# Row sums of a 16384 x 1024 array: the last eight rows as five runs instead of four, with pieces of two rows summed on ScalarE

## The chip, the cores and the metric

The kernel runs on one core of a Trainium2 chip. The time is what the device takes for one execution, in microseconds (us); the kernel before takes 160.38 us, the median of three runs (160.38 to 160.41). A profile is one such execution, recorded instruction by instruction; its span runs from the first to the last instruction of the program.

Three engines of the core matter here. VectorE (DVE in the profile) and ScalarE (ACT) do the sums; SyncE (SP) issues the loads and the last store. Each engine works through its own instructions in order and waits on semaphores; a DMA adds 16 to its semaphore once all of it has landed. TensorE (PE) and GpSimd (POOL) do nothing for the result.

## The reference

```
def setup_inputs():
    batch, seq, dim = 32, 512, 1024
    return {"x": np.random.randn(batch, seq, dim).astype(np.float32)}

def reference(x):
    return np.sum(x, axis=-1).astype(np.float32)
```

64 MiB are read, and one number is kept of each row of 1024 values: 16384 sums, 64 KiB.

## The kernel before

**Tiling.** The 16384 rows are spread over 128 partitions, 128 rows to each (`J`). They are cut into two regions of the array: the first 16 rows of every partition (`x_a`, `out_a`), and the other 112 (`x_b`, `out_b`). Within a region each partition's rows are contiguous in memory. `sums` holds one column for each of the 128 rows of a partition.

**Loads.** All are issued by SyncE (L99). The first load has 8 rows a partition (4 MB); it is moved to the very start of the program by `issue_first_load_at_entry`. Then come seven blocks of 16 rows (8 MB each) into three buffers in turn (L150 to L155). From the third block on, SyncE waits with `summed` until the block that used the buffer has been reduced (L153). The last eight rows, called rows 0 to 7 below, wait in the same way (L176) and then come as four runs, each a contiguous stretch of every partition's 8192 values (L178 to L183):

| run | values | what | goes to |
|---|---|---|---|
| 1 | 5632 | rows 0 to 4, left half of row 5 | buffer |
| 2 | 1792 | row 6, the first 768 values of row 7 | buffer, at its seventh row |
| 3 | 512 | right half of row 5 | `ends` |
| 4 | 256 | the last 256 values of row 7 | `ends` |

**Sums.** `vec` (L104) is one VectorE reduction over a whole block; the first load and blocks 0 to 5 are done so (L173 to L175). `halves` (L113) sums one stretch on VectorE: it adds the two halves of the stretch pair by pair and accumulates the result, so a row of 1024 is one operation of 512 pairs, followed by a short instruction that writes the accumulated sum. `act` (L129) sums one stretch on ScalarE: an activation that copies to PSUM (never read again, four places in turn, so that an activation waits for the fourth one before it) with an accumulated sum, and again a short instruction that writes the sum. Each adds one to `acts`.

Block 6, the last whole one, is divided: its first ten rows are summed by VectorE with `halves` (L193 to L195), its other six by ScalarE (L196, L197). Then the last eight rows:

- VectorE waits for run 1, sums the left half of row 5 into a column right behind the place of run 3 (L201, `carried`), and then rows 0, 1 and 2. It waits for run 2 and sums row 7's first 768 values into a column behind the place of run 4 (L218). Then it waits for run 3 and sums it with that column (257 pairs: 512 values, the carried sum, a zero) for row 5 (L221), and waits for run 4 and does the same for row 7 (129 pairs, L224), which sets `done`.
- ScalarE sums rows 3 and 4 out of run 1 and row 6 out of run 2 (L204 to L206). Behind these it waits for block 6's sums and for run 2, and issues two stores of all earlier sums (L212, L213).
- SyncE waits for `done` and for all of ScalarE's sums (L227, L228), stores the last 16 columns of `sums` (L229), and waits until they have landed; that ends the program.

There is no scheduler: the order on each engine is the order in which the function writes it.

Of the kernel before, what the change touches and what calls it, by code (L numbers as in the profile page):

```python
# [29 lines left out]
@with_exitstack  # L30
def kernel(
    ctx: ExitStack,
    tc: tile.TileContext,
    x: bass.AP,
    out: bass.AP,
):
    nc = tc.nc
    nc.at_finalize(issue_first_load_at_entry)

    tc.close()
    tc.compile()  # L43

    fp32 = mybir.dt.float32
    P = 128
    batch, seq, dim = x.shape
    rows = batch * seq
    J = rows // P
    BIG = 16  # L50
    x_r = x.flatten_outer_dims()
    out_r = out.rearrange("b s -> (b s)")
    ONE = BIG
    TWO = J - ONE

    def region(first, n):
        lo, hi = first * P, (first + n) * P
        return (
            x_r[lo:hi, :].rearrange("(p j) d -> p j d", j=n),
            out_r[lo:hi].rearrange("(p j) -> p j", j=n),  # L60
        )

    x_a, out_a = region(0, ONE)
    x_b, out_b = region(ONE, TWO)

    def rows_from(j, n):
        if j < ONE:
            return x_a[:, j : j + n, :]
        return x_b[:, j - ONE : j - ONE + n, :]

    last = J // BIG - 1
    tail = last * BIG
    FIRST = 8

    taken = (nc.sbuf_base + 31) // 32 * 32
    ctx.enter_context(nc.sbuf_tensor("unused", [P, -taken % 4096], mybir.dt.uint8))
    bufs = [
        ctx.enter_context(nc.sbuf_tensor(f"rows_{k}", [P, BIG * dim], fp32))
        for k in range(3)
    ]  # L80
    SIXTH, EIGHTH = 512, 768
    PAD = 64
    ends = ctx.enter_context(
        nc.sbuf_tensor("ends", [P, 2 * (dim + PAD) - SIXTH - EIGHTH], fp32)
    )
    sums = ctx.enter_context(nc.sbuf_tensor("sums", [P, J], fp32))
    unread = [
        ctx.enter_context(nc.psum_tensor(f"unread_{k}", [P, dim], fp32)) for k in range(4)
    ]

    def semaphore(name):
        return ctx.enter_context(nc.semaphore(name=name))

    def block_of(t, a, n):
        return t[:, a * dim : (a + n) * dim].rearrange("p (n d) -> p n d", d=dim)

    def load(dst, src, k):
        sem = semaphore(f"load_{k}")
        nc.sync.dma_start(out=dst, in_=src).then_inc(sem, 16)  # L99
        return sem  # L100

    summed = semaphore("summed")

    def vec(j, block):  # L104
        n = block.shape[1]
        return nc.vector.tensor_reduce(  # L106
            out=sums[:, j : j + n],
            in_=block,
            axis=mybir.AxisListType.X,
            op=mybir.AluOpType.add,  # L110
        )

    def halves(dst, src):  # L113
        n = src.shape[-1] // 2
        return nc.vector.tensor_tensor_reduce(  # L115
            out=src[:, :n],
            in0=src[:, :n],
            in1=src[:, n:],
            scale=1.0,
            scalar=0.0,  # L120
            op0=mybir.AluOpType.add,
            op1=mybir.AluOpType.add,
            accum_out=dst,
        )

    acts = semaphore("acts")
    n_acts = 0

    def act(j, src, landed=None):  # L129
        nonlocal n_acts  # L130
        if landed is not None:
            nc.scalar.wait_ge(landed, 16)
        if n_acts >= len(unread):
            nc.scalar.wait_ge(acts, n_acts - len(unread) + 1)
        nc.scalar.activation(  # L135
            out=unread[n_acts % len(unread)][:, :],
            in_=src,
            func=mybir.ActivationFunctionType.Copy,
            accum_out=sums[:, j : j + 1],
        ).then_inc(acts, 1)  # L140
        n_acts += 1

    t = bufs[0]
    block = block_of(t, 0, FIRST)
    landed = load(block, rows_from(tail, FIRST), "first")
    loads = [(landed, tail, block)]
    for g in range(last):  # L150
        t = bufs[(1 + g) % 3]
        if g > 1:
            nc.sync.wait_ge(summed, g - 1)  # L153
        block = block_of(t, 0, BIG)
        loads.append((load(block, rows_from(g * BIG, BIG), g), g * BIG, block))  # L155

    j = tail + FIRST
    t = bufs[(1 + last) % 3]

    rows5, left6 = block_of(t, 0, 5), t[:, 5 * dim : 5 * dim + SIXTH]
    c = 6 * dim
    row7, left8 = t[:, c : c + dim], t[:, c + dim : c + dim + EIGHTH]
    n6, n8 = dim - SIXTH, dim - EIGHTH
    right6, right8 = ends[:, :n6], ends[:, n6 + PAD : n6 + PAD + n8]
    whole6, whole8 = ends[:, : n6 + 2], ends[:, n6 + PAD : n6 + PAD + n8 + 2]
    left_sums = [w[:, -2:-1] for w in (whole6, whole8)]  # L170
    for w in (whole6, whole8):
        nc.vector.memset(w[:, -1:], 0.0)  # L172
    for landed, first, block in loads[:-1]:  # L173
        nc.vector.wait_ge(landed, 16)
        vec(first, block).then_inc(summed, 1)  # L175
    nc.sync.wait_ge(summed, last - 1)  # L176
    line = rows_from(j, 8).rearrange("p n d -> p (n d)")
    runs = ((t[:, : 5 * dim + SIXTH], 0), (t[:, c : c + dim + EIGHTH], 6 * dim),  # L178
            (right6, 5 * dim + SIXTH), (right8, 7 * dim + EIGHTH))
    five, seventh, sixth, eighth = (  # L180
        load(dst, line[:, at : at + dst.shape[-1]], f"run_{k}")
        for k, (dst, at) in enumerate(runs)
    )  # L183

    def sum_of(row):
        return sums[:, j + row : j + row + 1]

    paired = semaphore("paired")
    carried = semaphore("carried")
    landed, first, block = loads[-1]  # L190
    n_pairs = 10
    nc.vector.wait_ge(landed, 16)
    for q in range(n_pairs):  # L193
        op = halves(sums[:, first + q : first + q + 1], block[:, q, :])
    op.then_inc(paired, 1)  # L195
    for q in range(n_pairs, BIG):  # L196
        act(first + q, block[:, q, :], landed if q == n_pairs else None)  # L197
    n_early = n_acts

    nc.vector.wait_ge(five, 16)  # L200
    halves(left_sums[0], left6).then_inc(carried, 1)  # L201
    for q in range(3):
        halves(sum_of(q), rows5[:, q, :])
    for q in range(3, 5):  # L204
        act(j + q, rows5[:, q, :], five if q == 3 else None)
    act(j + 6, row7, seventh)  # L206

    early = semaphore("early")
    nc.scalar.wait_ge(acts, n_early)
    nc.scalar.wait_ge(paired, 1)  # L210
    nc.scalar.wait_ge(seventh, 16)
    nc.scalar.dma_start(out=out_b[:, : TWO - BIG], in_=sums[:, ONE : J - BIG]).then_inc(early, 16)  # L212
    nc.scalar.dma_start(out=out_a, in_=sums[:, :ONE]).then_inc(early, 16)  # L213
    nc.scalar.wait_ge(early, 32)

    done = semaphore("done")
    nc.vector.wait_ge(seventh, 16)
    halves(left_sums[1], left8).then_inc(carried, 1)  # L218
    nc.vector.wait_ge(sixth, 16)
    nc.vector.wait_ge(carried, 1)  # L220
    halves(sum_of(5), whole6)  # L221
    nc.vector.wait_ge(eighth, 16)
    nc.vector.wait_ge(carried, 2)
    halves(sum_of(7), whole8).then_inc(done, 1)  # L224

    stored = semaphore("stored")
    nc.sync.wait_ge(done, 1)  # L227
    nc.sync.wait_ge(acts, n_acts)  # L228
    nc.sync.dma_start(out=out_b[:, TWO - BIG :], in_=sums[:, J - BIG :]).then_inc(stored, 16)  # L229
    nc.sync.wait_ge(stored, 16)  # L230
# [30 lines left out]
```

## Time and profile before

| | us |
|---|---|
| median of three runs | 160.38 |
| the profiled execution | 160.36 |
| its span, first to last instruction | 159.0 (159.05) |
| VectorE busy | 121.7 |
| ScalarE busy | 10.9 |
| block 6 landed | 147.47 |
| VectorE's first and last operation on the last eight rows | 154.15, 157.48 |
| last store: issued, landed | 157.59, 159.01 |

The groups of operations by shape, VectorE's and then ScalarE's (the columns after the bar are busy time in us, the mean of one in ns, and idle time before them with what ended it):

```profile
L106 DVE TENSOR_REDUCE sums<-rows 128x16 f32<-128x16384 f32 x6 | 103.3, 17220 | 21.3 <-DMA rows<-in_x_dram 21.3
...
L115 DVE CUSTOM_DVE_ANT_0 rows<-rows 128x512 f32<-128x512 f32 x13 | 8.1, 689 | 2.2 <-DMA rows<-in_x_dram 2.2
```

```profile
L135 ACT ACTIVATE unread<-rows 128x1024 f32<-128x1024 f32 x9 | 9.1, 1014 | 145.1 <-DMA rows<-in_x_dram 145.1
L135 ACT ACTIVATION_READ_ACCUMULATOR unread<-rows 128x1 f32 x9 | 1.7, 187 | 0.0
```

In a timeline each line has the start in us, the length in us, the engine, the line of the kernel, the operation, and what it writes and reads; in square brackets stands how long the engine was idle before it, and what ended the wait. An engine with a q behind its name (SPq, ACTq) is that engine's issuing side. Operations of one engine can overlap a little: the next one starts while the one before it still writes. CUSTOM_DVE_ANT_0 is `halves`, ACTIVATE is `act`, and the READ_ACCUMULATOR behind each writes its sum.

### The profile page before, as it was taken

To read this page: it belongs to the slowest core of one execution; us is meant where nothing else is said; L and a number is where in the kernel's file an instruction comes from. 1 tells how busy PE (TensorE), PEld (TensorE's weight loads), DVE (VectorE), ACT (ScalarE), POOL (GpSimd) and SP (SyncE) were. 2 spreads that over 40 slices of the span, in tenths; PEclk is the share of its full clock that TensorE was granted. 3 is DMA by queue.
4 is the path that set the end of the run, shared out by engine and by line. 5 is a ranking of instruction groups with operands and counts; after the bars stand their busy time and mean duration, and the time that the engine had idled before them with its cause. 6 is when DMAs were issued, how large, how long until landed. Compare 5 with 4: busy or idle time off the path is not lost.

```text
span 159.0 us, 124 instructions
## 1 busy us (share of the span) xinstructions
DVE 121.7 (77%) x43; ACT 10.9 (7%) x19; POOL 0.2 (0%) x4
## 2 busy tenths in 40 slices
DVE  0009920199994999949999599986999679995986
ACT  3000000000000000000000000000000000000995
POOL 0000000000000000000000000000000000000000
DMA  7996996997989969969969969989799699698994
GB/s 264 478 577 264 527 527 264 527 445 346 527 379 412 527 280 511 527 264 527 527 264 527 511 280 527 429 363 527 313 478 527 264 527 527 264 527 354 425 394 162
DMA packets 2160, 67.18 MB, mean 422 GB/s; under 512 B 624, under 2 KB 752, under 8 KB 1008
## 3 DMA queue, kind: packets, MB, share of 16 engines
q1 hardware_dynamic: 1872, 67.12, 98.1%
q10 hardware_dynamic: 288, 0.06, 0.2%
HBM read 67.11 MB, written 0.07 MB: 422 GB/s over the span
## 4 chain that ended last, share of the span: by engine, by line
DMA 74%; DVE 24%; issue 0%; SPq 0%
DMA rows<-in_x_dram 74%; DVE sums L106 22%; DVE rows L115 2%; SPq L99 0%; DVE ends L115 0%; DVE sums L115 0%
## 5 line engine op out<-in xcount | busy, mean ns | idle before, releaser
L106 DVE TENSOR_REDUCE sums<-rows 128x16 f32<-128x16384 f32 (+1 forms) x7 | 112.0, 16001 | 31.7 <-DMA rows<-in_x_dram 31.7
L135 ACT ACTIVATE unread<-rows 128x1024 f32<-128x1024 f32 x9 | 9.1, 1014 | 145.1 <-DMA rows<-in_x_dram 145.1
L115 DVE CUSTOM_DVE_ANT_0 rows<-rows 128x512 f32<-128x512 f32 (+2 forms) x15 | 8.9, 662 | 2.6 <-DMA rows<-in_x_dram 2.6
L135 ACT ACTIVATION_READ_ACCUMULATOR unread<-rows 128x1 f32 x9 | 1.7, 187 | 0.0
L135 ACT ACT_TABLE_LOAD x1 | 1.3, 1283 | 1.4 <-PEq L43 1.4
L115 DVE DVE_READ_ACCUMULATOR2_ANT sums<- 128x1 f32 x15 | 1.3, 84 | 0.0
L172 DVE MEMSET ends<- 128x1 f32 x2 | 0.1, 59 | 1.5 <-PEq L43 1.5
L115 DVE CUSTOM_DVE_ANT_0 ends<-ends 128x257 f32<-128x257 f32 (+1 forms) x2 | 0.6, 360 | 0.0
L115 DVE DVE_READ_ACCUMULATOR2_ANT ends<- 128x1 f32 x2 | 0.2, 83 | 0.0
L245 POOL MEMSET const-bfloat16-1.0<- 128x1 bf16 x1 | 0.1, 101 | 0.0
L245 POOL MEMSET const-uint8-127<- 128x1 uint8 x1 | 0.1, 101 | 0.0
L245 POOL MEMSET const-float32-0.0<- 128x1 f32 x1 | 0.1, 98 | 0.2 <-issue 0.2
L245 POOL MEMSET const-float32-1.0<- 128x1 f32 x1 | 0.1, 98 | 0.0
## 6 DMA issues: line engine op xcount, KB each, us to landing
rows<-in_x_dram SPq DMA_DIRECT2D x1, 4096.0 KB, 12.0
rows<-in_x_dram SPq DMA_DIRECT2D x1, 2816.0 KB, 28.1
rows<-in_x_dram SPq DMA_DIRECT2D x1, 896.0 KB, 29.9
ends<-in_x_dram SPq DMA_DIRECT2D x1, 256.0 KB, 30.1
ends<-in_x_dram SPq DMA_DIRECT2D x1, 128.0 KB, 29.8
rows<-in_x_dram SPq DMA_DIRECT2D x7, 40.8
out_dram<-sums ACTq DMA_DIRECT2D x1, 48.0 KB, 1.6
out_dram<-sums ACTq DMA_DIRECT2D x1, 8.0 KB, 1.5
```

Source lines behind the costliest of these rows:

```text
L106: return nc.vector.tensor_reduce(out=sums[:, j : j + n], in_=block, axis=mybir.AxisListType.X, op=mybir.AluOpType.add,)
L115: return nc.vector.tensor_tensor_reduce(out=src[:, :n], in0=src[:, :n], in1=src[:, n:], scale=1.0, scalar=0.0, op0=mybir.AluOpType.add, op ...
L135: nc.scalar.activation(out=unread[n_acts % len(unread)][:, :], in_=src, func=mybir.ActivationFunctionType.Copy, accum_out=sums[:, j : j + ...
L172: nc.vector.memset(w[:, -1:], 0.0)
L245: nc = _bacc.Bacc("TRN2", target_bir_lowering=False, num_devices=1)
```

## The change

The last eight rows are cut into five runs, which are no longer in the order of the rows:

| run | values | what | goes to |
|---|---|---|---|
| A | 5376 | right half of row 2, rows 3 to 6, the first 768 values of row 7 | buffer |
| B | 1728 | row 0, the first 704 values of row 1 | buffer, at its seventh row |
| C | 640 | the last 128 values of row 1, left half of row 2 | `ends` |
| D | 256 | the last 256 values of row 7 | `ends` |
| E | 192 | the 192 values of row 1 between the two other pieces | `ends` |

VectorE takes out of run A the right half of row 2 and rows 3, 5 and 6; then row 0 (run B), the rest of row 2 with its carried sum (run C, 257 pairs), the rest of row 7 (run D, 129 pairs), and the rest of row 1 (run E, 97 pairs).

ScalarE sums row 7's first 768 values (run A) into the column behind run D's place, row 4 (run A), row 1's first 704 values (run B) and its last 128 (run C) into the two columns behind run E's place. So VectorE waits for `acts` before row 7's rest and again before row 1's rest. `act` takes the place of its sum as an argument instead of a row's number, and writes as many values to PSUM as it reads.

ScalarE's two early stores no longer wait for the second run; in its queue they stand behind the four sums.

```diff
-    SIXTH, EIGHTH = 512, 768
     PAD = 64
+    SECOND, LAST, FIRSTS = 512, 256, 192
+    THIRD = 128 + SECOND
     ends = ctx.enter_context(
-        nc.sbuf_tensor("ends", [P, 2 * (dim + PAD) - SIXTH - EIGHTH], fp32)
+        nc.sbuf_tensor("ends", [P, THIRD + LAST + FIRSTS + 3 * PAD], fp32)
     )
...
-    def act(j, src, landed=None):
+    def act(dst, src, landed=None):
...
-            out=unread[n_acts % len(unread)][:, :],
+            out=unread[n_acts % len(unread)][:, : src.shape[-1]],
...
-            accum_out=sums[:, j : j + 1],
+            accum_out=dst,
...
+    c1, c2, c7 = dim - FIRSTS - 128, SECOND, dim - LAST
+    spans = (
+        (2 * dim + c2, 7 * dim + c7),
+        (0, dim + c1),
+        (dim + c1 + FIRSTS, 2 * dim + c2),
+        (7 * dim + c7, 8 * dim),
+        (dim + c1, dim + c1 + FIRSTS),
+    )
+    size = [hi - lo for lo, hi in spans]
+    at3, at4, at5 = 0, THIRD + PAD, THIRD + PAD + LAST + PAD
+    B0 = 6 * dim
+    dsts = (
+        t[:, : size[0]],
+        t[:, B0 : B0 + size[1]],
+        ends[:, at3 : at3 + size[2]],
+        ends[:, at4 : at4 + size[3]],
+        ends[:, at5 : at5 + size[4]],
+    )
+    a2 = dim - c2
+    right2, row = t[:, :a2], [t[:, a2 + q * dim : a2 + (q + 1) * dim] for q in range(4)]
+    left7 = t[:, a2 + 4 * dim : size[0]]
+    row0, left1 = t[:, B0 : B0 + dim], t[:, B0 + dim : B0 + size[1]]
+    right1 = ends[:, at3 : at3 + 128]
+    whole2 = ends[:, at3 + 128 : at3 + THIRD + 2]
+    whole7 = ends[:, at4 : at4 + LAST + 2]
+    whole1 = ends[:, at5 : at5 + FIRSTS + 2]
...
-    nc.vector.wait_ge(five, 16)
-    halves(left_sums[0], left6).then_inc(carried, 1)
-    for q in range(3):
-        halves(sum_of(q), rows5[:, q, :])
-    for q in range(3, 5):
-        act(j + q, rows5[:, q, :], five if q == 3 else None)
-    act(j + 6, row7, seventh)
+    nc.vector.wait_ge(run_a, 16)
+    halves(whole2[:, -2:-1], right2).then_inc(carried, 1)
+    for q, k in ((3, 0), (5, 2), (6, 3)):
+        halves(sum_of(q), row[k])
+    act(whole7[:, -2:-1], left7, run_a)
+    n_seventh = n_acts
+    act(sum_of(4), row[1])
+    act(whole1[:, -2:-1], left1, run_b)
+    act(whole1[:, -1:], right1, run_c)
...
-    nc.scalar.wait_ge(seventh, 16)
...
-    nc.vector.wait_ge(seventh, 16)
-    halves(left_sums[1], left8).then_inc(carried, 1)
-    nc.vector.wait_ge(sixth, 16)
+    nc.vector.wait_ge(run_b, 16)
+    halves(sum_of(0), row0)
+    nc.vector.wait_ge(run_c, 16)
     nc.vector.wait_ge(carried, 1)
-    halves(sum_of(5), whole6)
-    nc.vector.wait_ge(eighth, 16)
-    nc.vector.wait_ge(carried, 2)
-    halves(sum_of(7), whole8).then_inc(done, 1)
+    halves(sum_of(2), whole2)
+    nc.vector.wait_ge(acts, n_seventh)
+    nc.vector.wait_ge(run_d, 16)
+    halves(sum_of(7), whole7)
+    nc.vector.wait_ge(acts, n_acts)
+    nc.vector.wait_ge(run_e, 16)
+    halves(sum_of(1), whole1).then_inc(done, 1)
```

More of the change, by code (lines that the diff above doesn't have):

```diff
@@ L162 @@
     t = bufs[(1 + last) % 3]
[L164 to L171, printed above, removed]
+    c1, c2, c7 = dim - FIRSTS - 128, SECOND, dim - LAST
[24 more added lines that the diff above has]
+    whole1 = ends[:, at5 : at5 + FIRSTS + 2]
+    for w in (whole2, whole7):
         nc.vector.memset(w[:, -1:], 0.0)
@@ L177 @@
     line = rows_from(j, 8).rearrange("p n d -> p (n d)")
[L178 to L183, printed above, removed]
+    landed_runs = [
+        load(dst, line[:, lo:hi], f"run_{k}") for k, (dst, (lo, hi)) in enumerate(zip(dsts, spans))
+    ]
+    run_a, run_b, run_c, run_d, run_e = landed_runs
     def sum_of(row):
@@ L196 @@
     for q in range(n_pairs, BIG):
-        act(first + q, block[:, q, :], landed if q == n_pairs else None)
+        act(sums[:, first + q : first + q + 1], block[:, q, :], landed if q == n_pairs else None)
     n_early = n_acts
-    nc.vector.wait_ge(five, 16)
-    halves(left_sums[0], left6).then_inc(carried, 1)
-    for q in range(3):
-        halves(sum_of(q), rows5[:, q, :])
-    for q in range(3, 5):
-        act(j + q, rows5[:, q, :], five if q == 3 else None)
-    act(j + 6, row7, seventh)
+    nc.vector.wait_ge(run_a, 16)
[7 more added lines that the diff above has]
+    act(whole1[:, -1:], right1, run_c)
     early = semaphore("early")
```

## The prediction

> **What bounds the kernel now.** I read the page first (busy shares, then the chain that ended last), and after it the last 6 us of the trace.
>
> ```profile
> DVE 121.7 (77%) x43; ACT 10.9 (7%) x19; POOL 0.2 (0%) x4
> ...
> DMA 74%; DVE 24%; issue 0%; SPq 0%
> ```
>
> VectorE is busy for 77% of the span, yet three quarters of the chain is the arrival of rows: the kernel follows its loads until the last run is in. The second 24% is mostly two early reductions that hold a buffer, and the change doesn't touch them. What it can move is the piece from the landing of block 6 (147.47 us, when L194 and L197 start) to the end at 159.05. The chain by time shows that piece:
>
> ```profile
> 125.98 28.14 DMA rows<-in_x_dram
> ...
> 154.15 0.43 DVE rows L115
> ...
> 156.92 0.04 DVE ends L115
> 156.96 0.31 issue
> 157.27 0.08 DVE sums L115
> 157.35 0.21 DVE ends L115
> ```
>
> The first of four runs lands at 154.13, VectorE works without a break from there, and the end follows VectorE. Next the four runs, as the page has their issues (the last column is the time to landing):
>
> ```profile
> rows<-in_x_dram SPq DMA_DIRECT2D x1, 2816.0 KB, 28.1
> rows<-in_x_dram SPq DMA_DIRECT2D x1, 896.0 KB, 29.9
> ends<-in_x_dram SPq DMA_DIRECT2D x1, 256.0 KB, 30.1
> ends<-in_x_dram SPq DMA_DIRECT2D x1, 128.0 KB, 29.8
> ```
>
> They are issued at 125.98, 126.35, 126.84 and 127.37; their semaphores fill at 154.13, 156.24, 156.89 and 157.21. So they queue behind one another: 6.65, 2.12, 0.65 and 0.32 us for 5632, 1792, 512 and 256 values a partition. The rest is the timeline of VectorE, then that of ScalarE with its DMA issues, then SyncE's last store:
>
> ```profile
> 153.63 0.08 DVE L115 DVE_READ_ACCUMULATOR2_ANT sums<- 128x1 f32 x1
> 154.15 0.43 DVE L115 CUSTOM_DVE_ANT_0 rows<-rows 128x256 f32<-128x256 f32 x1 [0.44 <-DMA rows<-in_x_dram]
> ...
> 156.92 0.43 DVE L115 CUSTOM_DVE_ANT_0 ends<-ends 128x257 f32<-128x257 f32 x1
> ...
> 157.27 0.29 DVE L115 CUSTOM_DVE_ANT_0 ends<-ends 128x129 f32<-128x129 f32 x1
> 157.48 0.08 DVE L115 DVE_READ_ACCUMULATOR2_ANT sums<- 128x1 f32 x1
> ```
>
> ```profile
> 156.27 1.03 ACT L135 ACTIVATE unread<-rows 128x1024 f32<-128x1024 f32 x1
> 156.35 0.37 ACTq L212 DMA_DIRECT2D out_dram<-sums  x1
> 156.75 0.46 ACTq L213 DMA_DIRECT2D out_dram<-sums  x1
> 157.23 0.19 ACT L135 ACTIVATION_READ_ACCUMULATOR unread<-rows 128x1 f32 x1
> ```
>
> ```profile
> 157.59 0.35 SPq L229 DMA_DIRECT2D out_dram<-sums  x1
> ```
>
> VectorE could have taken its next work at 153.71 and waited to 154.15. After that it ran almost gapless; run 3 held it for 0.1 us (156.82 to 156.92), run 4 was in 0.06 us before its operation began. Three limits (loads, VectorE, ScalarE at 157.42) end within 0.15 us of each other.
>
> **The change, part by part.** *Loads.* The same 8192 values, so the same stream, cut elsewhere. Run A (5376): 6.65 x 5376/5632 = 6.35, in at 147.47 + 6.35 = 153.83. Run B (1728): 2.12 x 1728/1792 = 2.04, at 155.87. Run C (640): the 512 and 256 runs differ by 0.33 for 256 values, so 0.65 + 0.16 = 0.81, at 156.68. Run D (256): 0.32, at 157.00. Run E (192) has no row: the line through 512 and 256 gives 0.24, and it shouldn't take longer than 256 values, 0.32; I take 0.25, next to the line: 157.25 (157.24 to 157.32). The fifth issue is another 0.45 us of SyncE near 127.8, hidden by the 26 us that block 6 and run A still need; without that cover it would be 0.45. The last values thus come 0.04 later than now.
>
> *VectorE.* An operation starts 0.02 after its landing (154.13 to 154.15). Starts are 0.61 apart at 512 pairs and 0.35 at 256 or 257; at 129 the accumulator read follows after 0.21. From 257 to 129 that is 0.14 for 128 pairs, so 97 pairs take 0.21 - 0.035 = 0.18. Start 153.85; right half of row 2: 154.20; rows 3, 5 and 6: 156.04; row 0 (B has been in for 0.17): 156.65; rest of row 2 waits for C, 156.70 to 157.05; rest of row 7 (D in at 157.00): 157.05 to 157.27; rest of row 1 with E: starts at 157.27, both free and landed. Then 0.18, the read 0.08, 0.03 to SyncE's issue: 157.56 against 157.59. VectorE has 0.31 us more work (512 pairs for 384, and the 97), paid by the start 0.30 earlier. The two waits on `acts` that now stand in its queue hold what is behind them, rows 7 and 1 and then the store; that of row 7 is met near 154.8, so only the last counts.
>
> *ScalarE.* All its rows are 1024 wide: 1.01 long, 1.04 from start to start, 1.03 after a wait, the accumulator read starting 0.065 before the end and lasting 0.19. Narrower ones are bounded by a time in proportion (128: 0.13) and by no saving at all (1.03). I go by VectorE's rows: 129 pairs take 0.29 and 257 take 0.43, so 0.15 is fixed. With 0.15 of ScalarE's 1.01 fixed, 768, 704 and 128 take 0.79, 0.74 and 0.26. Row 7's left part starts at 153.85, row 4 at 154.69, row 1's left part waits for B (155.89) and frees the engine at 156.68; the 128 values start with C at 156.70, and their sum is written at 157.10, seen at 157.13. VectorE asks for it at 157.27: 0.14 to spare. By the Trainium skill (ScalarE: Activation LUTs, What ACT_TABLE_LOAD costs) an ACTIVATE with immediate operands is 186 ns + 0.833 N, an estimate of 0.29 us at 128; the sum would not change, and no run here shows that width yet.
>
> *Stores.* ScalarE's two early stores lose the wait for run 2 but now stand behind the 128 values, which wait for C: 156.70 + 0.08 (as 156.27 to 156.35 now) = 156.78, and the second at 157.18. Loads have left the queue by then. The second lands 1.52 after its issue: 158.70, 0.3 before the last store, so ScalarE's wait on them costs nothing; past 159.0 it would set the end.
>
> **Sum.** 157.56 - 157.59 = -0.03. The profiled execution took 160.36 (span 159.05, and 1.31 around it, unchanged), so 160.33; the median of the runs is 0.02 above that execution: 160.35. A difference under 0.2% (0.32 us) counts as none here.
>
> **Rivals.** *Collision: the last store meets an early one.* Now the second early store's issue ends at 157.21, 0.38 before SyncE's. After the change it lasts from 157.18 to 157.64, and SyncE wants to issue at 157.56. For it: an issue alone took 0.33, but 0.44 to 0.48 right behind another. Against it: those were on one engine; two engines never issue together in this trace. Price: 0.08 of waiting and 0.11 of slower issue, 160.35 + 0.19 = 160.54. The Trainium skill (Perfetto Trace Analysis, DMA Instruction — HWDGE) says the descriptor generator is shared and locked by one sequencer at a time; no run here shows that so far, and by it this rival would happen.
>
> *Late sum, slower than before: ScalarE's last sum holds row 1.* The place is the wait for all sums in front of row 1. It decides once the 128 values take more than 0.28 + 0.14 = 0.42. With 0.60 fixed they take 0.65 and the 704 take 0.89: start 156.81, sum seen at 157.62, 0.35 late, 160.70. With no saving at all, row 4 ends at 155.95, the 704 at 157.01, and the sum is seen at 158.19: 161.27. For it: no narrow ScalarE row exists here. Against it: VectorE's rows shrink nearly with their width.
>
> *Dear runs: a fifth one costs the stream more.* Runs of 512 and 256 took 1.27 and 1.25 ns a value, the long one 1.18: 0.05 and 0.02 lost. Twice the larger loss on each of C, D and E would put E at most 0.2 later, 160.55.
>
> *Faster by 0.2%.* At the long run's 1.18 ns a value the last run lands at 157.15, but VectorE is busy to 157.27 anyway. So nothing below about 160.30 follows from this trace; 0.2% would need a stream faster than any seen.
>
> **How the numbers follow.** Forecast 0.58; collision 0.25; dear runs 0.06; late sum 0.08; faster 0.03. The first three lie within 0.2% of 160.38: same 0.89, slower 0.08, faster 0.03. The range runs from that floor of 160.30 with a margin of 0.03 (profiled against median) to past collision and dear runs, a good half of the way on to the late sum's first price: 160.27 to 160.64.
>
> **What would show it.** Landings at 153.83, 155.87, 156.68, 157.00 and 157.25, each within 0.05; VectorE's only waits before run A and C; the 128-wide ACTIVATE near 0.26; the last issue at 157.56 and 0.35 long (0.46 would be the collision). Wrong would be a gap in front of the 97 pairs with run E long in (late sum), or landings that drift by 0.1 a run (dear runs).

## The result, and the profile after

The changed kernel takes 160.76 us (median of 9 runs, 160.69 to 161.32), the kernel before beside it on the same chip 160.37 (9 runs, 160.29 to 160.57). The ratio is 1.0029, with a 95% interval of 1.0019 to 1.0040: slower by 0.3%, a little over the 0.2% from which a difference counts here, and outside the range that was given.

Busy time and the chain of the changed kernel's page look as before:

```profile
DVE 122.1 (77%) x45; ACT 10.8 (7%) x21; POOL 0.2 (0%) x4
...
DMA 74%; DVE 24%; issue 0%; SPq 0%
```

The runs on the same page (KB, and us from issue to landing):

```profile
rows<-in_x_dram SPq DMA_DIRECT2D x1, 2688.0 KB, 27.8
rows<-in_x_dram SPq DMA_DIRECT2D x1, 864.0 KB, 29.5
ends<-in_x_dram SPq DMA_DIRECT2D x1, 320.0 KB, 29.8
ends<-in_x_dram SPq DMA_DIRECT2D x1, 128.0 KB, 29.7
...
ends<-in_x_dram SPq DMA_DIRECT2D x1, 96.0 KB, 29.4
```

By the times at which their semaphores fill the runs A to E land at 153.80, 155.84, 156.64, 157.04 and 157.28. ScalarE's and SyncE's ends in the timeline:

```profile
156.66 0.28 ACT L136 ACTIVATE unread<-ends 128x128 f32<-128x128 f32 x1
156.72 0.37 ACTq L228 DMA_DIRECT2D out_dram<-sums  x1
156.88 0.19 ACT L136 ACTIVATION_READ_ACCUMULATOR unread<-ends 128x1 f32 x1
157.12 0.46 ACTq L229 DMA_DIRECT2D out_dram<-sums  x1
```

```profile
157.71 0.35 SPq L248 DMA_DIRECT2D out_dram<-sums  x1
```

and VectorE's:

```profile
156.66 0.43 DVE L116 CUSTOM_DVE_ANT_0 ends<-ends 128x257 f32<-128x257 f32 x1
157.02 0.08 DVE L116 DVE_READ_ACCUMULATOR2_ANT sums<- 128x1 f32 x1
157.17 0.29 DVE L116 CUSTOM_DVE_ANT_0 ends<-ends 128x129 f32<-128x129 f32 x1
157.39 0.08 DVE L116 DVE_READ_ACCUMULATOR2_ANT sums<- 128x1 f32 x1
157.42 0.26 DVE L116 CUSTOM_DVE_ANT_0 ends<-ends 128x97 f32<-128x97 f32 x1
```

Run C's operation starts 0.02 after its landing, but D's starts at 157.17 and E's at 157.42, each 0.13 after its own. The last store goes out at 157.71 instead of 157.59, and the span is 159.16 instead of 159.05: 0.11 of the loss. The profiled execution, however, took 160.75 instead of 160.36, which is 0.39 more. So 0.28 lies where no line of the profile is: time less span was 1.31 and is 1.59. (Spans with two decimals are from the trace; the page has 159.2 and 159.0.)

### The profile page after: what moved, and what is told of

The parts are those of the page before. It is cut to its first block, busy times and chain, and to the rows that moved or that the text cites. A ratio compares the mean times of both kernels' runs of the same rounds, so it can differ in the third digit from the quotient of the medians.

```text
span 159.2 us, 131 instructions
## 1 busy us (share of the span) xinstructions
DVE 122.1 (77%) x45; ACT 10.8 (7%) x21; POOL 0.2 (0%) x4
## 4 chain that ended last, share of the span: by engine, by line
DMA 74%; DVE 24%; issue 0%; SPq 0%
DMA rows<-in_x_dram 74%; DVE sums L107 22%; DVE rows L116 2%; DVE ends L116 0%; SPq L100 0%; DVE sums L116 0%
## 5 line engine op out<-in xcount | busy, mean ns | idle before, releaser
L136 ACT ACTIVATE unread<-rows 128x1024 f32<-128x1024 f32 (+2 forms) x9 | 8.6, 961 | 144.8 <-DMA rows<-in_x_dram 144.8
L116 DVE CUSTOM_DVE_ANT_0 rows<-rows 128x512 f32<-128x512 f32 (+1 forms) x15 | 9.1, 670 | 2.3 <-DMA rows<-in_x_dram 2.2
L116 DVE CUSTOM_DVE_ANT_0 ends<-ends 128x257 f32<-128x257 f32 (+2 forms) x3 | 0.9, 328 | 0.1
```

The lines of the kernel that those rows point to most:

```text
L116: return nc.vector.tensor_tensor_reduce(out=src[:, :n], in0=src[:, :n], in1=src[:, n:], scale=1.0, scalar=0.0, op0=mybir.AluOpType.add, op ...
L136: nc.scalar.activation(out=unread[n_acts % len(unread)][:, : src.shape[-1]], in_=src, func=mybir.ActivationFunctionType.Copy, accum_out=ds ...
```

## The experiments

Three theories were on the table at first: ScalarE's early stores, which landed 0.37 later (158.65), set the end (stores theory); the program's size costs something outside the span (size theory); VectorE's late last operations are the loss (wait theory).

**s1, early stores in front of the last activation.**

```diff
+    (the two early stores, with their two waits)
     act(whole1[:, -1:], right1, run_c)
-    (the two early stores, with their two waits)
     nc.scalar.wait_ge(early, 32)
```

> The changed kernel, with ScalarE's two early stores issued in front of its last activation (the 128 values of row 1) instead of behind it. In the changed kernel they are issued at 156.73 and 157.13 and have landed at 158.65, 0.37 later than before, and the time grew by 0.39 though the span grew by only 0.11. Stores theory (ScalarE's last landing sets the end of the execution, not SyncE's): they are issued near 155.95, land 0.7 to 0.8 earlier, and the time falls by 0.25 to 0.45 us, to 160.3 to 160.5. Size theory (one more load, semaphore and a few instructions cost 0.28 outside the span): no change, 160.75. Wait theory (the whole loss is VectorE's late last two operations): no change, 160.75.

160.80, ratio 1.0027 (1.0017 to 1.0037). The stores landed at 157.77, 0.88 earlier, and it gained nothing: 1.58 outside the span.

**s2, the kernel before with its early stores held back.**

```diff
-    nc.scalar.wait_ge(seventh, 16)
+    nc.scalar.wait_ge(sixth, 16)
```

> The kernel before, with ScalarE's early stores held back until run 3 (156.89) instead of run 2 (156.24) has landed. Stores theory: issue 0.6 to 0.7 later, time up by about as much, near 161.0, with most of it outside the span. Size theory and wait theory: no change, 160.37, unless SyncE's last store waits for the issue of ScalarE's, which would be seen in the span (0.1 to 0.25).

160.43, 1.0003 (0.9994 to 1.0013), 1.32 outside. The stores landed at 158.91. Here the second one was being issued from 157.38 to 157.83 when SyncE issued its last, at 157.58; that issue took 0.35 as ever, though it landed 1.50 later instead of 1.42. The stores theory has fallen, and the collision of two issues cost 0.08 here.

**s3, the waits exchanged in the changed kernel.**

```diff
-    nc.vector.wait_ge(acts, n_seventh)
     nc.vector.wait_ge(run_d, 16)
+    nc.vector.wait_ge(acts, n_seventh)
...
-    nc.vector.wait_ge(acts, n_acts)
     nc.vector.wait_ge(run_e, 16)
+    nc.vector.wait_ge(acts, n_acts)
```

> The changed kernel, with VectorE's waits on a run and on ScalarE's sums exchanged for rows 7 and 1, so that the wait on the run comes first in the text. In the changed kernel the wait on the run is an instruction of its own, and the operations begin 0.13 after the landing, against 0.02 to 0.03 before. Wait theory: both begin within 0.03 of their landing or of VectorE being free, the last store is issued 0.1 to 0.15 earlier (near 157.58) and the time falls by as much, to 160.62. Stores theory: the span falls by as much, but the time stays within 0.05 of 160.75, because ScalarE's stores set it. Size theory: as the wait theory, with 1.59 outside the span.

160.69, 1.0019 (1.0009 to 1.0029), 1.58 outside. VectorE in the timeline of s3:

```profile
157.09 0.29 DVE L116 CUSTOM_DVE_ANT_0 ends<-ends 128x129 f32<-128x129 f32 x1
157.31 0.08 DVE L116 DVE_READ_ACCUMULATOR2_ANT sums<- 128x1 f32 x1
157.33 0.26 DVE L116 CUSTOM_DVE_ANT_0 ends<-ends 128x97 f32<-128x97 f32 x1
```

Runs D and E landed at 157.07 and 157.31, so both operations now start 0.02 behind their run. The wait theory holds for the span; the median fell by 0.07, which the intervals can't tell from nothing.

**s4, the kernel before with a fifth run and fill.**

```diff
+    (in words) three memsets on VectorE, one activation of 4 values on ScalarE, semaphore "filled",
+    a wait for the fifth run on VectorE and one on ScalarE
-    runs = ((t[:, : 5 * dim + SIXTH], 0), ...
+    runs = ((t[:, : 4 * dim], 0), (t[:, 4 * dim : 5 * dim + SIXTH], 4 * dim), ...
```

> The kernel before, with its run 1 loaded as two runs on two semaphores (4096 and 1536 values), and with three memsets on VectorE, one tiny activation on ScalarE and one semaphore more, all at the start where the engines are idle. It has the fifth run and at least as many instructions as the changed kernel, but its stores and its last operations stand as before. Size theory: about 0.28 more outside the span, 160.65. Stores theory and wait theory: within 0.1 of the kernel before.

160.84, 1.0034 (1.0021 to 1.0047), 1.71 outside. The old arithmetic with more program loses more than the change does, so it is something of the program's size. The next four took its parts singly, each added to the kernel before (v3 and v4 in words):

```diff
v1  +    op.then_inc(semaphore("extra"), 1)                      # on a memset that is there
v2  +    for k in range(3): nc.vector.memset(spare[:, k : k + 1], 0.0)
v3  +    run 1 as two DMAs on one semaphore, waits for 32
v4  +    two activations of 8 values, behind the landing of block 5
```

> The kernel before with one semaphore more and nothing else (VectorE's second memset at the start also adds 1 to a semaphore that nobody waits for). The time outside the span (time of the profiled execution less its span) was 1.31 in the kernel before, 1.59 in the changed kernel (one semaphore more) and 1.71 in the kernel before with a fifth run and fill (two more). Semaphore theory: about 1.5 to 1.6 outside the span, time near 160.6. Instruction theory (VectorE's instructions count: 3 more in the changed kernel, 4 in the filled one) and load theory: 1.31, 160.36.

160.33, 1.0001 (0.9987 to 1.0015), 1.32 outside: not the semaphore.

> The kernel before with three more memsets on VectorE at the start, where it waits 12 us for the first load, and nothing else. Instruction theory for VectorE: 0.09 outside the span for each, so 1.58, time near 160.63. Semaphore theory and load theory: 1.31, 160.36.

160.55, 1.0010 (1.0000 to 1.0020), 1.58 outside: three memsets, hidden near 1.5 us, while VectorE waits for the first load, cost what the whole change costs outside the span.

> The kernel before with run 1 loaded as two DMAs (4096 and 1536 values) on one semaphore, so one DMA more and neither a semaphore nor an instruction of another engine more. Load theory: about 0.27 more outside the span, 160.63. The others: 1.31, 160.36 to 160.45 (a second DMA may move the landings by 0.02 to 0.05).

160.39, 0.9999 (0.9987 to 1.0010), 1.31 outside: not the load.

> The kernel before with two tiny activations more on ScalarE, near 128 us where it is idle, and nothing else. Instruction theory for ScalarE (2 more in the changed kernel, 1 more in the filled one): up to 0.28 more outside the span. Semaphore, load and VectorE theories: 1.31, 160.36.

160.34, 0.9997 (0.9985 to 1.0008), 1.31 outside: not ScalarE.

So it goes with VectorE's instructions: counted in the built program, waits and barriers among them, 52 in the kernel before, 55 in the changed one and in v2, 56 in s4. Two theories were left: a price for each, or an edge.

**b1, two VectorE instructions fewer in the kernel before.**

```diff
-    for w in (whole6, whole8):
-        nc.vector.memset(w[:, -1:], 0.0)
+    nc.vector.memset(ends[:, :], 0.0)
...
     for q in range(3):
+        if q == 2:
+            nc.vector.wait_ge(carried, 1)
         halves(sum_of(q), rows5[:, q, :])
...
     nc.vector.wait_ge(sixth, 16)
-    nc.vector.wait_ge(carried, 1)
```

> The kernel before with two VectorE instructions fewer and the same work: one memset over the whole of ends in place of two, and the wait on the first carried sum moved to an operation that has no wait (row 2), so that it needs no instruction of its own. Count theory (each VectorE instruction costs 0.09 to 0.1 us outside the span): outside 1.31 - 0.18 = 1.13, time 160.18. Step theory (the cost begins only beyond some number of instructions between 52 and 55): 1.31, 160.36.

160.42, 1.0004 (0.9995 to 1.0013), 1.31 outside. No price for each: my count theory was wrong.

**b2, twelve memsets more** (v2 with `range(12)`).

> The kernel before with twelve more memsets on VectorE at the start, where it waits for the first load. Three gave 0.27 outside the span. Count theory: 12 x 0.09 = 1.08 more, outside 2.39, time near 161.45. Step theory: as with three or four, 0.3 to 0.4 more, near 160.7.

161.04, 1.0043 (1.0028 to 1.0058). Neither theory had this: 1.32 outside, but a span of 159.91. The DMA view of the whole kernel before has no queue q14, and that of b2 has (queue, packets, MB, share; then the last store with its us to landing):

```profile
q14 instruction: 1, 0.01, 0.0%
...
out_dram<-sums SPq DMA_DIRECT2D x1, 8.0 KB, 2.1
```

and the same line in the DMA view of the kernel before, from 157.9 us on:

```profile
out_dram<-sums SPq DMA_DIRECT2D x1, 8.0 KB, 1.4
```

One packet of 8192 bytes of instructions ran from 158.43 to 158.94, while the last store's packets began at 158.65. Of that store's 144 packets 135 had started by 158.84; the other nine, one sixteenth, started from 158.93 on, as the instruction packet ended. A DMA's sixteen increments come one by one: here fifteen came by 159.24, the last at 159.88. So the store landed 2.08 after its issue instead of 1.42, which is 0.66 of the longer span; the rest is loads that came in 0.2 later.

**b3, the last store held back.**

```diff
     nc.sync.wait_ge(acts, n_acts)
+    nc.sync.wait_ge(early, 32)
```

> The kernel before with SyncE's last store held until ScalarE's early stores have landed (158.28), 0.7 after VectorE's last operation, whose time stays. The span grows by about 0.7, to 159.75. If what VectorE's instructions cost is added behind the whole program, or ahead of it, the time outside the span stays 1.31 and the time is near 161.08. If it runs beside the last store, from VectorE's end on, the time outside shrinks by as much as the span grows, and the time stays near 160.4 to 160.6.

161.09, 1.0046 (1.0031 to 1.0061). The span grew to 159.90, with 1.31 outside: what lies outside the span doesn't shrink when SyncE ends later.

**b4, the changed kernel with 52 VectorE instructions.**

```diff
-    for w in (whole2, whole7):
-        nc.vector.memset(w[:, -1:], 0.0)
+    nc.vector.memset(ends[:, :], 0.0)
...
+    nc.vector.wait_ge(carried, 1)
     halves(sum_of(5), row[2])
+    nc.vector.wait_ge(acts, n_seventh)
     halves(sum_of(6), row[3])
...
     nc.vector.wait_ge(run_c, 16)
-    nc.vector.wait_ge(carried, 1)
     halves(sum_of(2), whole2)
-    nc.vector.wait_ge(acts, n_seventh)
     nc.vector.wait_ge(run_d, 16)
     halves(sum_of(7), whole7)
-    nc.vector.wait_ge(acts, n_acts)
     nc.vector.wait_ge(run_e, 16)
+    nc.vector.wait_ge(acts, n_acts)
```

> The changed kernel with VectorE's instructions back at the number of the kernel before (52 in place of 55), and the same work: one memset over ends in place of two, the waits on the carried sum and on row 7's left part moved to rows 5 and 6, which have no wait, and the wait on run E put first. Count theory with wait theory: outside 1.31, last store issued near 157.57, span 159.0, time 160.3 to 160.4, which is the kernel before. If only the wait order mattered: 160.6 to 160.65, outside 1.59.

160.39 against 160.32 of the kernel before, 1.0007 (0.9998 to 1.0016), 1.32 outside. VectorE's end in its timeline:

```profile
156.97 0.29 DVE L116 CUSTOM_DVE_ANT_0 ends<-ends 128x129 f32<-128x129 f32 x1
157.19 0.08 DVE L116 DVE_READ_ACCUMULATOR2_ANT sums<- 128x1 f32 x1
157.19 0.26 DVE L116 CUSTOM_DVE_ANT_0 ends<-ends 128x97 f32<-128x97 f32 x1
```

Run E landed at 157.16, and the last operation follows VectorE's own work without a gap, as forecast. With both costs gone the five runs are as fast as the four within what can be told, and no faster.

**c1, c2 and c8, one, two and eight memsets more in the kernel before** (v2 with `range(1)`, `range(2)`, `range(8)`).

> The kernel before with one memset more on VectorE at the start: 53 instructions in its program. Fetch theory (VectorE's program reaches the next block of its instructions shortly behind the last store; 52 is still short of it, 55 and 56 are past it by 0.27 and 0.39 us): if each instruction past an edge costs 0.09 to 0.12 and the edge is at 52, 0.09 more outside the span, 1.40 and 160.45; if the edge is at 53 or 54 with a jump, 1.31 and 160.36.

160.39, 0.9996 (0.9984 to 1.0008), 1.32 outside.

> The kernel before with two memsets more: 54 instructions. Edge at 52 with 0.09 each: 1.49 outside the span, 160.54. A jump at 55: 1.31 and 160.36; a jump at 53 or 54: near 1.58 and 160.6.

160.34, 0.9998 (0.9988 to 1.0008), 1.31 outside. With v2 (1.58) the edge stands between 54 and 55.

> The kernel before with eight memsets more: 60 instructions. With twelve more the trace shows one more 8192-byte packet of the runtime's queue at 158.43, inside the span, the last store's landing 0.65 later than usual and 1.32 outside the span. Fetch theory: the block is asked for later in the program the fewer instructions there are, so with eight the packet comes between 158.4 and the end or just after the span, and the loss is 0.4 to 0.8, in the span if the packet is in it and otherwise outside (160.8 to 161.1). Count theory: 8 x 0.09 = 0.7 outside, always.

160.60, 1.0012 (1.0002 to 1.0022), 1.73 outside, a span of 159.03. The instruction packet is there again, as the DMA view from 160 to 161 us shows, 40 slices of 0.025 us:

```profile
DMA  0000000000000000900000000000000000000000
...
q14 instruction: 1, 0.01, 3.6%
```

It starts at 160.41, behind the span and two microseconds later than with four instructions more. That it would come later is what the fetch theory had, but the time is below the 160.8 to 161.1 that I gave: the loss is 0.42 in the profiled execution and 0.27 between the medians, and it is not steady, since the time outside the span went from 1.3 to 1.8 over the nine executions. Nor is it shown that this packet makes the loss: by its 3.6% of 16 engines over 1 us it lasts 0.58 us, to 160.99, and the execution took 160.76.

| VectorE instructions | kernels | outside the span, us |
|---|---|---|
| 50 | b1 | 1.31 |
| 52 | before, s2, v1, v3, v4, b3, b4, w1 | 1.31 to 1.32 |
| 53, 54 | c1; c2, d1 | 1.32; 1.31, 1.31 |
| 55 | changed, s1, s3, v2 | 1.58 to 1.59 |
| 56, 60 | s4, c8 | 1.71, 1.73 |
| 64 | b2 | 1.32, with 0.66 in the last store |

The table has the profiled executions. Of the others the span is on record to 0.1 us, so that each value is good to 0.05, and they say the same: 1.26 to 1.36 outside in each of 220 executions with 50 to 54 instructions (119 of them of the kernel before), 1.53 to 1.63 in all 35 with 55, 1.69 to 1.75 in all five with 56. So it is no price for each instruction, and more than one step: s4 is another 0.13 above 55, though s4 differs from the kernel before in more than their number.

**w1, the order of waits by itself, in the kernel before.**

```diff
-    nc.vector.wait_ge(sixth, 16)
     nc.vector.wait_ge(carried, 1)
+    nc.vector.wait_ge(sixth, 16)
...
-    nc.vector.wait_ge(eighth, 16)
     nc.vector.wait_ge(carried, 2)
+    nc.vector.wait_ge(eighth, 16)
```

> The kernel before with VectorE's waits on the carried sums put in front of the waits on runs 3 and 4, so that the waits on the runs become instructions of their own. The same number of instructions (52), the same loads and sums. Wait theory: run 3's operation begins 0.13 after its landing instead of 0.02, VectorE's last two operations and the last store come 0.1 to 0.15 later (with run 4's landing covered by run 3's operation, or a second 0.1 if not), outside the span 1.31, time 160.45 to 160.6. If the order of waits is nothing: 160.36.

160.47, 1.0009 (1.0000 to 1.0019), 1.31 outside. Run 3 landed at 156.88; the operation that waits for it, in VectorE's timeline:

```profile
156.75 0.08 DVE L115 DVE_READ_ACCUMULATOR2_ANT ends<- 128x1 f32 x1
157.02 0.43 DVE L115 CUSTOM_DVE_ANT_0 ends<-ends 128x257 f32<-128x257 f32 x1 [0.19 <-DMA ends<-in_x_dram]
```

0.14 behind the landing, against 0.02 in the kernel before; the last store went out at 157.70, 0.10 later. Nothing but the order of the two waits was changed, in front of both operations.

**d1, the changed kernel with one VectorE instruction fewer** (b4's memset alone).

> The changed kernel with one memset over the whole of ends in place of its two on single columns, and nothing else: 54 VectorE instructions in place of 55, its waits as they are. Edge theory (a jump between 54 and 55): 1.31 outside the span instead of 1.59, last store still 0.43 behind run E's landing (the two late operations stay), time 160.45 to 160.5. Count theory (0.09 for each): 1.50 outside, 160.66.

160.46, 1.0008 (0.9999 to 1.0017), 1.31 outside. One instruction at the start of VectorE's program is worth 0.28 of the 0.39 us by which the profiled executions differ; here the store was issued 0.42 behind run E's landing (0.43 in the changed kernel, 0.31 forecast), so the waits still cost their 0.11.

## Why the prediction was wrong, point by point

**Landings, right.** 153.80, 155.84, 156.64, 157.04 and 157.28 against 153.83, 155.87, 156.68, 157.00 and 157.25. Run E took 0.24 (0.25 taken), run D 0.40 instead of 0.32, the one that was short. The rival of dear runs is out. The prediction's three limits, though, do not end within 0.15 us of each other: the last landing before is at 157.21, and VectorE's end, 157.56, is 0.35 behind it.

**ScalarE, right.** The 128 values took 0.28, where 0.26 was estimated, the 704 and 768 took 0.76 and 0.82. By the Trainium skill (ScalarE: Activation LUTs, What ACT_TABLE_LOAD costs) an ACTIVATE with immediate scale and bias takes 186 ns + 0.833 N, an estimate of 0.29, 0.77 and 0.83 for these three. The trace agrees to about 0.01. The sum was written at 157.07 (157.10 forecast), before VectorE asked for it: no late sum. (By the prediction's own numbers the sum would have been late from 0.26 + 0.14 = 0.40 on, not 0.42; nothing hung on that.)

**Early stores, right, and no collision.** Their second issue ended at 157.58, before SyncE's at 157.71, which took 0.35. In s2 the two did overlap, and SyncE's issue was no longer than alone; only the landing was 0.08 later. The Trainium skill (Perfetto Trace Analysis, DMA Instruction — HWDGE) says that the descriptor generator is shared and locked for one sequencer's use at a time. No such wait is to be seen in s2's issue.

**The first step that failed** is the one in VectorE's part that every operation starts 0.02 after its landing. That was measured on waits that ride on the operation itself, that is, are part of it. In these traces only the first written of two waits rides; the other stands in front as a wait instruction of its own. In the kernel before that was `carried`, long met; in the changed kernel it is the run, on which everything depends. So VectorE's waits before runs D and E, of which the prediction had none, cost 0.11 at run E (0.13 for 0.02): its wait instruction starts at 157.31, 0.03 behind the landing, and the operation another 0.11 later. s3 and w1 show it both ways. The changed order stands in the diff, which writes `acts` first. The Trainium skill (Perfetto Trace Analysis, Sequencer-only Instruction and DVE / Act Engine Instruction) has an engine's operation wait in a queue behind the sequencer, while an instruction of the sequencer alone keeps it from fetching the next one until its wait is met. The trace fits that; those sections state no time for it.

**The second, and larger, is the word "unchanged"** in the sum, for the 1.31 us around the span. It became 1.59. Shown: it hangs on the number of VectorE's instructions, jumps between 54 and 55 (v2, c2, d1), and goes with neither a semaphore, nor a load, nor ScalarE's instructions, nor when the stores end. Shown as well: with 60 and 64 instructions the instruction queue moves one more packet of 8192 bytes near the end. The Trainium skill (CRC Debugging, Comparing the Two Runs) counts queue 14 as the sequencers' instruction refills. The profile, too, names q14 "instruction".

How the number of instructions makes the 0.27 stays open. No trace with 55 or 56 instructions shows such a packet, and its times rather speak against it: it came 1.98 later with 60 instructions than with 64, so that at the same rate (an estimate from these two traces) it would come behind 162 us with 55 or 56, while the changed kernel's whole execution took 160.75. Nor is anything later that the trace records around the span. It also has semaphore updates that are not the kernel's own, from 0.38 us ahead of the first instruction to 1.43 behind the last, and in the changed kernel, v2 and s4 they stand, within 0.02 us, where they stand in the kernel before. Only c8 differs: one group of 51 comes 0.74 to 1.03 behind the last instruction instead of 0.30 to 0.62, later by about its 0.42, and still ahead of its packet, which starts 1.38 behind.

**The two together.** The last store went out 0.15 later than forecast (157.71 for 157.56: 0.11 of the wait, 0.03 of run E's landing), and 0.28 came around the span. On the forecast 160.35 that makes 160.78, against 160.76 measured. Either step alone would have stayed inside the range.

**The forecast of no change** holds for what the change does to loads and sums: b4 is at 1.0007 (0.9998 to 1.0016). The chances failed because all rivals were looked for inside the span, and none of them was the order of two waits.

## What to carry to other kernels

Subtract the span from the time in both kernels before looking for a cause: what differs there has no line in the profile, and a single instruction at an engine's start can make it (0.28 between the changed kernel and d1). Where an operation needs two waits (tried here on VectorE), write the one that is met last first, so that it rides on the operation, or hang the other on an earlier operation that has none. A tail in which the last landing and the ends of ScalarE and VectorE lie within 0.35 us (157.21, 157.42, 157.56) has little left to win by cutting it finer: with its two costs gone the change gained nothing (b4).

## What was not expected of the hardware

An instruction's place doesn't matter for this cost: v2's three memsets of 0.06 us, run at 1.5 us behind a barrier, cost outside the span what the changed kernel's three more instructions cost, which stand in its last microseconds (1.58 and 1.59). And a single 8 KB packet of instructions, 0.5 us long, held one sixteenth of an 8 KB store back, which fits one of the core's 16 DMA engines: the last increment came 0.64 us behind the other fifteen (159.24 to 159.88 in b2), and with it the end of the program. The later start of its packets is 0.15 of that at most; what made the rest is not shown.
